# Chunked scan, rotation and output projection of a hybrid attention/HGRN2 layer: where the states, the rotation pieces and the last stage's instructions stand in order

## The chip, the cores and the metric

One core of one Trainium2 chip. The metric is device time in microseconds (us). The kernel before takes 2008.44 us, the median of 3 runs (2007.12 to 2008.82).

## The reference

One layer on 2048 latent tokens and 256 context tokens, model width 1024, float32. One input projection feeds two head groups, differential attention and a bidirectional HGRN2; both are gated, concatenated, projected, and added to the input under a LayerNorm:

```python
h_lat = x * (1.0 + scale) + shift
aq, ak, av, ag, hq, hi, hff, hfb, hg = _project(h_lat, w_in)     # 9 groups of 512 columns
q, k = _apply_rope(aq, cos, sin), _apply_rope(ak, cos, sin)      # rotation, latent tokens
p = softmax(q k^T / 8);  w = p[:, :, 0] - lam * p[:, :, 1];  attn = _rms_norm(w v) * 0.8
# HGRN2, forward and backward over the tokens, sum of both
S_t = diag(f_t) S_{t-1} + k_t v_t^T;  o_t = S_t^T q_t
y = concat([attn * silu(ag), _rms_norm(o_f + o_b) * silu(hg)]) @ w_out
x = _layer_norm(2 ** 0.25 * x + gate * y)
```

## The kernel before

Every float32 product is made of three products of halves (`hh`/`hl`, `wh`/`wl`: a rounded copy and the remainder), so one 128x512 result of depth 1024 takes 8 x 3 = 24 matmuls of 512 columns. The program has four stages in the profiled execution: input projections from 0 to about 920 us, into which the forward scan is merged from about 250 us; the last `aq`/`ak`/`hg` projections merged with the backward scan, 920 to 1092 us; attention, 1092 to 1803 us; the output projection of the last 14 of 16 tiles of 128 tokens, 1803 us to the end (2006.6 us).

**Projection and rotation.** `project_cols` (L469) issues 24 matmuls (L478) per bank of four called `pd`, and yields after every three. `evac_cols` empties the bank on ScalarE (L521, or L565 for `aq`/`ak`) into tiles called `e`. For `aq`/`ak` the rotation follows: `evac_scores` (L541) does a product at once or puts it into `self.deferred`. Its closure `rest` (L579) holds seven VectorE operations (L580, L581, L583, and twice L550 and L551) with four stores. `flush` (L465) runs everything deferred at one point, halfway through the next bank's matmuls (L480).

**Scan.** `merge` runs three steps of the projection, 9 matmuls, and then one step of the scan. The latent tokens form 8 groups (`NGRP`) of 256 tokens for each of two pairs of heads. The forward part of a group (`hgrn_group`, L640) goes through seven levels, in each of which four matmuls (L694) read what VectorE left (L695, L702). For the backward direction it stores three tiles of 256 KB: the decayed queries `QB` (L712), the state increments `UB` (L739) and the forward outputs `OP` (L754). `hgrn_backward` (L756) loads the three again for each group, in falling order of the groups. A step makes two products (L769) with the state `Sb`, then the next state by `state` (L632, L636), and a second step does the same for the other chunk; in a third step VectorE adds the bank to the forward outputs (L774) and the sum is stored to `Od`. State tiles have two buffers for each name, the banks `pm` too.

**Output projection.** For tile t, `front` (L217) loads gates `G` and mixed heads `Od`, squares on ScalarE (L1231), reduces on VectorE (L1234), scales by `rs` on POOL (L1240), transposes on TensorE (L1248), gates, rounds and takes the remainder on VectorE, VectorE and POOL (L1249, L1250, L1251). `back` makes 48 matmuls (L1272) and the residual and LayerNorm (L1275 to L1301, the last on POOL). `run` calls them tile after tile; a scheduler sets each engine's order. All DMAs are issued from one queue (SP), stores and loads alike.

Of the kernel before, what the change touches and what calls it, by code (L numbers as in the profile page):

```python
# [29 lines left out]
P = 128  # L30
D = 1024
# [87 lines left out]
class Build:  # L119
# [217 lines left out]
    def project_rest(self, att):  # L337
# [13 lines left out]
        yield from self.project(LAST_UNITS[:4], [0, 1])  # L351
        self.scores_projected = True
# [112 lines left out]
    def flush(self):  # L465
        while self.deferred:
            self.deferred.pop(0)()

    def project_cols(self, u, w, b, hb):  # L469
# [3 lines left out]
        for ct in range(2):  # L473
            ps = self.acc()
            cs = slice(ct * P, ct * P + P)
            for k in range(KT):
# [3 lines left out]
                if k == KT // 2:  # L480
                    self.flush()
# [59 lines left out]
    def evac_scores(self, kind, i, b, ps, n):  # L541
# [7 lines left out]
        def split(x, spare, half):  # L549
            nc.vector.tensor_copy(out=spare, in_=x)  # L550
            nc.vector.tensor_tensor(out=x.bitcast(F32R), in0=x, in1=spare.bitcast(F32), op=ALU.subtract)  # L551
            for d, src in zip(dst, (spare, x)):
                self.store(d[u].rearrange("(g t j) n -> t g j n", t=2, j=32)[half][:, :, ts], src.bitcast(F32))

        if b == NBLK:
            x, spare = tile("e1").bitcast(F32), tile("e2")
            nc.scalar.copy(out=x, in_=ps)
            self.deferred.append(lambda: split(x, spare, half))
            return
# [19 lines left out]
        def rest():  # L579
            nc.vector.tensor_tensor(out=xf, in0=xf, in1=cos, op=ALU.mult)  # L580
            nc.vector.tensor_tensor(out=p1f, in0=p1f, in1=pf, op=ALU.subtract)  # L581
            split(p1f, p, 0)
            nc.vector.tensor_tensor(out=x1f, in0=x1f, in1=xf, op=ALU.add)  # L583
            split(x1f, x, 1)

        self.deferred.append(rest)


    def hgrn(self):
# [4 lines left out]
        self.tot_b = {}  # L594
# [7 lines left out]
        loaded, active, finished = [], [], set()  # L602
# [29 lines left out]
    def state(self, S, d, u, tot, U):  # L632

        n = self.hg.tile([P, 2, P], F32, name=f"S{d}{u}", bufs=2)
# [5 lines left out]
    def hgrn_group(self, u, i, S):  # L640
# [67 lines left out]
        if latent:  # L708
# [3 lines left out]
            self.store(self.QBd[u][i], qq[:, 1, :, :])  # L712
# [9 lines left out]
        for d in range(2):  # L722
# [5 lines left out]
            t = hg.tile([P, 2, 2, P], F32, name="U%d" % d)  # L728
# [10 lines left out]
        self.store(self.UBd[u][i], U[1])  # L739
# [12 lines left out]
        op = hg.tile([P, 2, 2, P], F32, name="op", bufs=1)  # L752
        nc.scalar.copy(out=op, in_=po)
        self.store(self.OPd[u][i], op)  # L754

    def hgrn_backward(self, u, i, S, n):  # L756
        nc, hg, ph = self.nc, self.hg, self.ph
        tile = lambda nm, bufs: hg.tile([P, 2, 2, P], F32, name=nm, bufs=bufs)
        tags = ((("hq", 3), ("hv", 3), ("fb", 3)), (("km", 2), ("A", 2), ("kk", 3)))[n % 2]
        qb, ub, op = (tile(*x) for x in tags)  # L760
        qb = qb.rearrange("p a b t -> p a (b t)")
        self.load(qb, self.QBd[u][i])
        self.load(ub, self.UBd[u][i])
        self.load(op, self.OPd[u][i])
# [330 lines left out]
class Output:  # L1095
    def __init__(self, b):
        self.b, self.nc = b, b.nc
        self.gated = {}

# [90 lines left out]
    def run(self, out):  # L1190
# [9 lines left out]
        for t in range(2):  # L1200
            for _ in self.backs[t]:
                pass
        for t in range(2, NT):
            for _ in range(5 if t + 2 < NT else 0):
                self.advance(t + 2)
            for n in self.back(t):
                if n == 1 and t + 1 < NT:
                    while self.advance(t + 1):
                        pass
# [109 lines left out]
```

## Time and profile before

| | |
|---|---|
| median of 3 runs | 2008.44 us |
| time of the profiled execution | 2008.39 us |
| span of the profiled execution | 2006.6 us |
| TensorE (PE) busy | 1901.3 us, 95% |
| VectorE (DVE) busy | 1426.1 us, 71% |
| ScalarE (ACT) busy | 903.4 us, 45% |
| POOL busy | 894.1 us, 45% |
| DMA | 286.95 MB, mean 143 GB/s |

A busy share is an average over the four stages. TensorE's idle time is what can be won, and it lies in a few places; so the place, the engine that released it, and the granted clock of that stretch are read together.

### The profile page before, as it was taken

How to read it: one execution, taken by the hardware profiler on the slowest of the kernel's cores; microseconds unless marked ns; L12 is line 12 of the kernel's file. 1: busy time of each engine (PE TensorE's matmuls, PEld its weight loads, DVE VectorE, ACT ScalarE, POOL GpSimd, SP SyncE). 2: the span in 40 equal slices, each digit the busy share in tenths (PEclk: the TensorE clock that was granted, in tenths of full speed). 3: DMA queues.
4: the chain of work that ended last, by engine and by line, in shares of the span. 5: the costliest groups of instructions: out<-in, count | busy, mean ns of one | idle time of the engine just before them, and what ended most of it. 6: DMA issues, size and time to landing. Idle time of an engine off the chain costs nothing.

```text
span 2006.6 us, 32053 instructions
## 1 busy us (share of the span) xinstructions
PE 1901.3 (95%) x11712; PEld 1686.6 (84%) x11712; DVE 1426.1 (71%) x3055; ACT 903.4 (45%) x1349; POOL 894.1 (45%) x663
## 2 busy tenths in 40 slices
PE   7999999999998999999879999999999999998897
PEld 5888988898787998877667999999999999887676
DVE  7763456546687465777544389999999999967778
ACT  5523222322222322322000079989988889842121
POOL 0000145335445343453100057778777776745543
PEclk9999999999999999999889999999999999999999
DMA  9895652442444633434557641242252121144442
GB/s 359 269 260 184 231 184 90 165 156 75 147 134 145 198 121 127 161 106 145 189 181 232 195 130 51 76 139 74 70 144 64 44 82 43 46 152 161 148 146 95
DMA packets 180205, 286.95 MB, mean 143 GB/s; under 512 B 16848, under 2 KB 109264, under 8 KB 178000
## 3 DMA queue, kind: packets, MB, share of 16 engines
q1 hardware_dynamic: 180048, 284.91, 44.5%
q8 instruction: 93, 1.52, 0.3%
q14 instruction: 64, 0.52, 0.1%
HBM read 187.85 MB, written 97.00 MB: 142 GB/s over the span
## 4 chain that ended last, share of the span: by engine, by line
PE 63%; DVE 14%; DMA 12%; issue 4%; ACT 3%; POOL 3%; SPq 1%; DVEq 0%; POOLq 0%; ACTq 0%
PE pd L478 16%; PE po L1060 9%; PE pd L497 8%; PE s L973 6%; PE s L974 6%; PE pt L1040 6%; PE pl L694 4%; DMA QLd<-e 2%; PE py L1272 2%; DVE wl L428 2%; DMA KLd<-e 1%; DVE wsh L368 1%; PE pm L726 1%; DMA wraw<-win 1%; DMA kh<-Od 1%
## 5 line engine op out<-in xcount | busy, mean ns | idle before, releaser
L988 DVE TENSOR_SCALAR_CACHE_REDUCE e<-s 128x512 f32<-128x512 f32 (+1 forms) x512 | 372.8, 751 | 31.7 <-PE s L974 31.2
L478 PE MATMUL pd<-hh,wl 128*128 128x512 f32 (+1 forms) x928 | 372.3, 401 | 3.2 <-ACT e L534 3.2
L478 PE MATMUL pd<-hh,wh 128*128 128x512 f32 (+1 forms) x928 | 355.6, 383 | 0.0
L478 PE MATMUL pd<-hl,wh 128*128 128x512 f32 (+1 forms) x928 | 355.5, 383 | 0.0
L1023 POOL TENSOR_TENSOR e<-e,e 128x768 f32<-128x768 f32 (+1 forms) x192 | 351.1, 1857 | 2.6 <-ACT e L1016 0.2
L997 ACT ACTIVATE e<-e,nm 128x2304 f32<-128x2304 f32 x128 | 286.5, 2238 | 2.4 <-DVE nm L992 2.1
L973 PE MATMUL s<-kh,q 128*128 128x512 f32 (+1 forms) x640 | 244.4, 388 | 1.2 <-DMA q<-QHd 0.9
L974 PE MATMUL s<-kl,q 128*128 128x512 f32 (+1 forms) x640 | 231.4, 371 | 0.0
L699 POOL TENSOR_TENSOR kk<-kk,fb 128x512 f32<-128x512 f32 x126 | 170.5, 1355 | 134.4 <-DMA kk<-KD 101.3
L478 PEld LDWEIGHTS pd<-hh,wh 128*128 128x128 f32 x928 | 176.7, 190 | 34.3
L478 PEld LDWEIGHTS pd<-hh,wl 128*128 128x128 f32 x928 | 177.6, 191 | 31.0 <-ACT e L534 3.6
L478 PEld LDWEIGHTS pd<-hl,wh 128*128 128x128 f32 x928 | 177.6, 191 | 27.3
L689 ACT COPY km<-kk 128x512 f32<-128x512 f32 x112 | 70.9, 634 | 262.7 <-POOL kk L699 173.9
L1040 PE MATMUL pt<-eye,e 128*128 128x128 f32 x1152 | 162.8, 272 | 4.0 <-DVE w3l L1047 1.9
L1018 POOL TENSOR_SCALAR e<-e,cf 128x1280 f32<-128x1280 f32 x64 | 86.3, 1348 | 177.3 <-ACT e L997 73.5
L705 POOL TENSOR_TENSOR fb<-fb 128x512 f32<-128x512 f32 (+4 forms) x126 | 83.2, 661 | 162.5 <-DVE qq L702 148.0
L1040 PEld LDWEIGHTS pt<-eye,e 128*128 128x128 f32 x1152 | 135.7, 140 | 22.9 <-POOL e L1023 3.1
L694 PE MATMUL pl<-qq,km 128*128 128x128 f32 x896 | 131.1, 291 | 25.2 <-DVE qq L702 22.9
L694 PEld LDWEIGHTS pl<-qq,km 128*128 128x128 f32 x896 | 122.4, 196 | 38.2 <-issue 26.4
L497 PE MATMUL pd<-wh,hl 128*128 128x256 f32 x512 | 149.2, 291 | 1.1 <-ACT wh L427 1.1
L497 PE MATMUL pd<-wl,hh 128*128 128x256 f32 x512 | 145.4, 284 | 0.3 <-DVE wl L428 0.3
L497 PE MATMUL pd<-wh,hh 128*128 128x256 f32 x512 | 145.2, 284 | 0.0
(276 smaller groups left out, 4354.6 us busy)
## 6 DMA issues: line engine op xcount, KB each, us to landing
wraw<-win SPq DMA_DIRECT2D x68, 512.0 KB
xst<-xT SPq DMA_DIRECT2D x24, 512.0 KB
fb<-FD SPq DMA_DIRECT2D x18, 512.0 KB
kk<-KD SPq DMA_DIRECT2D x18, 512.0 KB
kh<-KHd SPq DMA_DIRECT2D x16, 576.0 KB
wsh<-wshift SPq DMA_DIRECT2D x16, 512.0 KB
wsh<-wscale SPq DMA_DIRECT2D x16, 512.0 KB
FD<-e SPq DMA_DIRECT2D x32, 256.0 KB
```

What stands on the lines that cost most here:

```text
L478: nc.tensor.matmul(ps[:, 0:n], a[:, k, cs], r[:, k, :], start=(k == 0 and j == 0), stop=(k == KT - 1 and j == 2))
L497: nc.tensor.matmul(ps[:, t, :], a[:, k, ts], r[:, k, :], start=(t == 0 and k == 0 and j == 0), stop=(t == 1 and k == KT - 1 and j == 2))
L694: nc.tensor.matmul(pl[:, e, ch, :], km[:, e, ch * P:ch * P + P], qm, start=True, stop=True)
L699: nc.gpsimd.tensor_tensor(out=o, in0=o, in1=total(fb, 1, 0, c), op=ALU.mult)
L973: nc.tensor.matmul(ps[:, c:c + w], q[:, m, :], kh[m][:, a + c:a + c + w], start=True, stop=False)
L974: nc.tensor.matmul(ps[:, c:c + w], q[:, 2 + m, :], kl[:, a + c:a + c + w], start=False, stop=True)
L988: self.nc.vector.tensor_scalar(out=d[e][:, a:b], in0=d.pop(("s", m, i)), scalar1=1.0, scalar2=None, op0=ALU.mult, op1=ALU.max, accum_out=s ...
L997: self.nc.scalar.activation(out=e, in_=e, func=AF.Exp, bias=self.tiles[t]["nm%d" % m], scale=1.0, accum_out=self.small(t, "z%d" % m))
L1018: self.nc.gpsimd.tensor_scalar(out=e, in0=e, scalar1=d["cf"], scalar2=1.0, op0=ALU.mult, op1=ALU.mult)
L1023: self.nc.gpsimd.tensor_tensor(out=d["e0"][:, a:b], in0=d["e0"][:, a:b], in1=d["e1"][:, a:b], op=ALU.add)
L1040: self.nc.tensor.transpose(out=ps[:, k - a, :], in_=d["e0"][:, k * P:k * P + P], identity=self.b.eye)
L1060: nc.tensor.matmul(out, a[:, k - _GROUPS[g][0], :], w[:, :, k - _GROUPS[g][0], :], start=(op == self.value_ends[0] and k == k0 and j == 0) ...
```

## The change

First, `flush` takes a number: from the second of a bank's eight steps on, one deferred piece is run per step and all that is left at the last; the closure `rest` is cut into seven pieces. Second, group 7 (`NGRP - 1`), the last of the forward scan and the first of the backward, keeps its three tiles on chip: six stores and six loads of 256 KB go. A backward group makes both its states in a step of their own, then its four products in the next; the state tiles take turns between the names `Sf` and `Sb`, which gives four buffers. Third, the output projection's instructions of TensorE, ScalarE, VectorE and the SP queue are written in order: `tile` places the next tile's transposes after 12 and 18 of the tile's 48 matmuls. From tile 4 on ScalarE squares with an accumulator (eight times 128 columns) and scales (eight more), and rounds; VectorE takes the remainder and does the LayerNorm in two products of 1024 columns; POOL does nothing. The front of tiles 2 and 3 stays as it was.

```diff
-    def flush(self):
-        while self.deferred:
+    def flush(self, n=None):
+        for _ in range(len(self.deferred) if n is None else min(n, len(self.deferred))):
             self.deferred.pop(0)()
...
-                if k == KT // 2:
-                    self.flush()
+                if k > 0:
+                    self.flush(1 if k < KT - 1 else None)
...
-        self.deferred.append(rest)
+        self.deferred += [times(xf, xf, cos), times(p1f, p1f, pf, ALU.subtract), *split(p1f, p, 0),
+                          times(x1f, x1f, xf, ALU.add), *split(x1f, x, 1)]
...
+        name = d
+        if d == "b" and ("f", u, NGRP - 1) in self.finished:
+            name = "fb"[self.turns[u] // 2 % 2]
+            self.turns[u] += 1
+        n = self.hg.tile([P, 2, P], F32, name=f"S{name}{u}", bufs=2)
...
-        self.store(self.OPd[u][i], op)
+        if i < NGRP - 1:
+            self.store(self.OPd[u][i], op)
+        else:
+            self.kept[u] = qq[:, 1, :, :], U[1], op
...
+        if i == NGRP - 1:
+            qb, ub, op = self.kept[u]
...
+        yield
+        tb, before = self.tot_b[u, i], {}
+        for c in (1, 0):
+            before[c] = S["b", u]
+            if i > 0 or c > 0:
+                self.state(S, "b", u, [tb[:, e, c:c + 1] for e in range(2)], ub[:, c, :, :])
         yield
         ps = ph.tile([P, 2, 2, P], F32, name="pm")
         for c in (1, 0):
             for e in range(2):
-                nc.tensor.matmul(ps[:, c, e, :], qb[:, e, c * P:c * P + P], S["b", u][:, e, :], start=True, stop=True)
-            if i > 0 or c > 0:
-                tb = self.tot_b[u, i]
-                self.state(S, "b", u, [tb[:, e, c:c + 1] for e in range(2)], ub[:, c, :, :])
-            yield
+                nc.tensor.matmul(ps[:, c, e, :], qb[:, e, c * P:c * P + P], before[c][:, e, :], start=True, stop=True)
+        yield
...
+        with self.b.tc.manual_schedule(engines={nc.tensor.engine, nc.scalar.engine, nc.vector.engine, nc.sync.engine}):
...
+    def tile(self, t):
...
+        products(half)
+        if before:
+            next(before)
+        if nxt:
+            self.gates(t + 1, 0)
+        products(2)
+        if nxt:
+            self.gates(t + 1, 1)
+        if before:
+            next(before, None)
+        if last:
+            return
+        products(2)
+        if nxt:
+            self.rest(t + 1)
+        next(back)
+        if t + 2 < NT:
+            self.norms(t + 2)
+        if t + 3 < NT:
+            self.fetch(t + 3)
+        products(KT)
...
+        for i in range(2 * H):
+            nc.scalar.activation(out=sq[:, i, :], in_=o[:, i, :], func=AF.Square, accum_out=ms[:, i:i + 1])
+        nc.scalar.activation(out=ms, in_=ms, func=AF.Sqrt, scale=1.0 / P, bias=self.b.eps)
+        nc.vector.reciprocal(out=rs, in_=ms)
+        for i in range(2 * H):
+            nc.scalar.activation(out=o[:, i, :], in_=o[:, i, :], func=AF.Copy, scale=rs[:, i:i + 1])
```

**VectorE in the backward scan, groups 7 to 5.** `Sf`/`Sb` on the left are new states (each row does both heads), `hv` and `A` the loaded increments; `fb`, `kk`, `op` are the sums of a bank `pm` with the forward outputs, and rows with `e` and `xst` (the rotation's sines and cosines) the rotation. Before:

```order
L636 SCALAR_TENSOR_TENSOR Sb_8296<-Sb_8250,tb_7_7947,hv 128x128 x2
L774 TENSOR_TENSOR fb<-pm,fb 128x512
L636 SCALAR_TENSOR_TENSOR Sb_8392<-Sb_8296,tb_6_7255,hv 128x128 x2
L580 TENSOR_TENSOR e_8302<-e_8302,xst 128x512
L581 TENSOR_TENSOR e_8227<-e_8227,e_8303 128x512
L583 TENSOR_TENSOR e_8226<-e_8226,e_8302 128x512
L550 CAST e_8303<-e_8227 128x512
L550 CAST e_8302<-e_8226 128x512
L551 TENSOR_TENSOR e_8227<-e_8227,e_8303 128x512
L551 TENSOR_TENSOR e_8226<-e_8226,e_8302 128x512
L636 SCALAR_TENSOR_TENSOR Sb_8362<-Sb_8339,tb_7_8127,A 128x128 x2
L774 TENSOR_TENSOR kk<-pm,kk 128x512
```
Now:

```order
L641 SCALAR_TENSOR_TENSOR Sb_8431<-Sf_8316,tb_6_7428,A 128x128 x2
L641 SCALAR_TENSOR_TENSOR Sb_8374<-Sb_8371,tb_6_7255,hv 128x128 x2
L794 TENSOR_TENSOR op<-pm,op 128x512
L641 SCALAR_TENSOR_TENSOR Sf_8491<-Sb_8374,tb_5_6645,hv 128x128 x2
L559 TENSOR_TENSOR e_8284<-e_8284,xst 128x512
L559 TENSOR_TENSOR e_8216<-e_8216,e_8285 128x512
L559 TENSOR_TENSOR e_8215<-e_8215,e_8284 128x512
L556 CAST e_8285<-e_8216 128x512
L556 CAST e_8284<-e_8215 128x512
L553 TENSOR_TENSOR e_8216<-e_8216,e_8285 128x512
L553 TENSOR_TENSOR e_8215<-e_8215,e_8284 128x512
L641 SCALAR_TENSOR_TENSOR Sb_8434<-Sb_8431,tb_6_7428,A 128x128
```
The first states of a group no longer stand between its own products: `Sf_8491` (group 5) is ahead of the seven rotation rows that follow, where `Sb_8362` (group 7) stood behind them. On TensorE a group is 4 products and then 27 matmuls of the projection, where it was 2, 9, 2 and 18.

**VectorE in the forward scan, the run of seven rotation operations that ends just ahead of TensorE's wait at 553.73 us.** `A` and `qq` are the scan's rows that TensorE waits for. Before:

```order
L580 TENSOR_TENSOR e_4852<-e_4852,xst 128x512
L581 TENSOR_TENSOR e_4783<-e_4783,e_4853 128x512
L583 TENSOR_TENSOR e_4782<-e_4782,e_4852 128x512
L550 CAST e_4853<-e_4783 128x512
L550 CAST e_4852<-e_4782 128x512
L551 TENSOR_TENSOR e_4783<-e_4783,e_4853 128x512
L551 TENSOR_TENSOR e_4782<-e_4782,e_4852 128x512
L695 COPY_PREDICATED A<-masks,pl 128x512
L702 TENSOR_TENSOR qq<-qq,fb 128x2x64x4
```
Now:

```order
L559 TENSOR_TENSOR e_4852<-e_4852,xst 128x512
L559 TENSOR_TENSOR e_4783<-e_4783,e_4853 128x512
L559 TENSOR_TENSOR e_4782<-e_4782,e_4852 128x512
L556 CAST e_4853<-e_4783 128x512
L700 COPY_PREDICATED A<-masks,pl 128x512
L553 TENSOR_TENSOR e_4783<-e_4783,e_4853 128x512
L707 TENSOR_TENSOR qq<-qq,fb 128x2x64x4
L556 CAST e_4852<-e_4782 128x512
L556 CAST e_4908<-e_4907 128x256
L553 TENSOR_TENSOR e_4782<-e_4782,e_4852 128x512
```
The scan's two rows have moved up by three and by two of the seven operations; at the next run of seven the rows stand as before.

**POOL at the start of the last stage.** `e<-e,rs` is the scaling of tile 3, `q<-q,lnb` the end of tile 0's LayerNorm, and `kl`, `e` of 512 columns the remainders. Before:

```order
L1240 TENSOR_TENSOR kh_18211<-kh_18211,rs 128x1024
L1251 TENSOR_TENSOR kl_18339<-kh_18211,kl_18339 128x512 x2
L1240 TENSOR_TENSOR e_18297<-e_18297,rs 128x1024
L1301 TENSOR_TENSOR q_18038<-q_18038,lnb 128x1024
L1301 TENSOR_TENSOR e_18260<-e_18260,lnb 128x1024
```
Now:

```order
L1397 TENSOR_TENSOR kh_18193<-kh_18193,rs 128x1024
L1408 TENSOR_TENSOR kl_18321<-kh_18193,kl_18321 128x512 x2
L1458 TENSOR_TENSOR q_18020<-q_18020,lnb 128x1024
L1397 TENSOR_TENSOR e_18279<-e_18279,rs 128x1024
L1458 TENSOR_TENSOR e_18242<-e_18242,lnb 128x1024
```
The scaling of tile 3, on which its transposes wait, has moved behind the end of tile 0's LayerNorm; on TensorE those transposes now stand after 12 of tile 2's matmuls, and what stands behind them there comes later.

## Rows read from the trace of the kernel before

**Rows 1.** Busy time by stretch: length, PE, PEld, DVE, ACT, POOL, clock, DMA share, GB/s.

```profile
920.00:1092.00 172.00, 146.28 (x697) 121.75 (x696) 89.53 (x186) 15.55 (x27) 18.18 (x18) 0.92 0.60 194
960.00:970.00 10.00, 4.76 (x13) 3.98 (x14) 5.17 (x13) 0.60 (x1) 0.00 (x0) 0.50 0.66 230
1803.00:1999.00 196.00, 174.21 (x828) 142.04 (x825) 155.78 (x225) 37.59 (x54) 96.44 (x54) 0.97 0.43 142
1820.00:1827.00 7.00, 6.26 (x15) 4.95 (x16) 5.23 (x9) 2.74 (x4) 4.27 (x3) 0.52 0.52 158
```

**Rows 2.** Waits of PE: line waited for, us in total, times, longest us.

```profile
PE pl L694 <- DVE qq L702: 22.9, 14, 5.1
PE pm L769 <- DVE Sb L636: 15.1, 3, 9.3
PE py L1272 <- POOL e L1251: 14.3, 6, 5.4
...
PE pm L769 <- DVE fb L774: 7.2, 2, 6.0
```

**Rows 3.** PE's timeline, backward scan: start us, us, operation, idle before and releaser.

```profile
965.24 1.23 PE L769 MATMUL pm<-Sb,km 128*128 128x128 f32 x4 [9.31 <-DVE Sb L636]
...
1008.23 0.80 PE L769 MATMUL pm<-Sb,hq 128*128 128x128 f32 x2 [5.29 <-DVE Sb L636]
...
1029.39 1.22 PE L769 MATMUL pm<-Sb,hq 128*128 128x128 f32 x4 [6.03 <-DVE fb L774]
```

**Rows 4.** The chain that ended last, 925 to 1095 us: start us, us, what.

```profile
954.53 10.28 DMA A<-UB
...
993.30 13.19 DMA QLd<-e
```

**Rows 5.** ACT's timeline, backward scan.

```profile
1006.59 1.09 ACT L565 ACTIVATE e<-pd 128x512 f32<-128x512 f32 x2 [18.11 <-DMA QLd<-e]
```

**Rows 6.** DVE's timeline in the forward scan.

```profile
549.80 2.58 DVE L551 TENSOR_TENSOR e<-e,e 128x512 fp32r<-128x512 f32 x2
552.30 0.71 DVE L695 COPY_PREDICATED A<-masks,pl 128x512 f32<-128x512 uint32 x1
```

**Rows 7.** PE's timeline, same place.

```profile
553.73 1.62 PE L694 MATMUL pl<-qq,km 128*128 128x128 f32 x6 [5.09 <-DVE qq L702]
```

**Rows 8.** PE's timeline, starts of tiles 3, 6, 7 and 15.

```profile
1820.74 0.79 PE L1272 MATMUL py<-woh,e 128*128 128x512 f32 x1 [5.35 <-POOL e L1251]
...
1861.86 0.50 PE L1272 MATMUL py<-woh,kl 128*128 128x512 f32 x1 [1.80 <-POOL kl L1251]
...
1876.05 0.50 PE L1272 MATMUL py<-woh,e 128*128 128x512 f32 x1 [1.99 <-POOL e L1251]
...
1987.10 0.28 PE L1272 MATMUL py<-woh,e 128*128 128x256 f32 x1
```

**Rows 9.** POOL's timeline, start of the last stage.

```profile
1805.66 1.90 POOL L1240 TENSOR_TENSOR e<-e,rs 128x1024 f32<-128x1024 f32 x1 [3.49 <-DVE rs L1239]
1808.86 2.38 POOL L1301 TENSOR_TENSOR q<-q,lnb 128x1024 f32<-128x1024 f32 x1 [1.30 <-DMA Od<-oa]
```

**Rows 10.** DVE's timeline, same stretch.

```profile
1807.40 1.24 DVE L1300 TENSOR_TENSOR q<-q,lng 128x1024 f32<-128x1024 f32 x1 [1.88 <-DMA lng<-lng]
```

**Rows 11.** ACT's groups, attention: shapes, count, then busy us, mean ns, idle before.

```profile
L997 ACT ACTIVATION_READ_ACCUMULATOR e<-e,nm 128x1 f32 x128 | 25.9, 203 | 0.0
...
L1081 ACT ACTIVATE oa<-pt,rz 128x128 f32<-128x128 f32 x62 | 19.3, 369 | 1.7 <-PE pt L1077 1.7
...
L1121 ACT CAST woh<-G 128x512 fp32r<-128x512 f32 x8 | 4.9, 607 | 0.0
```

**Rows 12.** All engines' groups, 1840 to 1990 us, same columns.

```profile
L1276 DVE SCALAR_TENSOR_TENSOR y<-x,y 128x512 f32<-128x512 f32 x22 | 29.1, 1324 | 0.4
...
L1300 DVE TENSOR_TENSOR y<-y,lng 128x1024 f32<-128x1024 f32 x11 | 13.5, 1226 | 14.7 <-ACT y L1299 14.7
...
L1249 DVE TENSOR_TENSOR e<-pt,G 128x512 f32<-128x512 f32 x12 | 8.2, 679 | 0.0
```

More of the change, by code (lines that the diff above doesn't have):

```diff
@@ L549, in split, with lower, times @@
         def split(x, spare, half):
[L550 to L553, printed above, removed]
+            def lower():
+                nc.vector.tensor_tensor(out=x.bitcast(F32R), in0=x, in1=spare.bitcast(F32), op=ALU.subtract)
+                for d, src in zip(dst, (spare, x)):
+                    self.store(d[u].rearrange("(g t j) n -> t g j n", t=2, j=32)[half][:, :, ts], src.bitcast(F32))
+            return [lambda: nc.vector.tensor_copy(out=spare, in_=x), lower]
+        def times(out, a, b, op=ALU.mult):
+            return lambda: nc.vector.tensor_tensor(out=out, in0=a, in1=b, op=op)
         if b == NBLK:
@@ L1098, in __init__ @@
         self.gated = {}
+        self.late = {}
     def open(self, stack):
@@ L1199, in run @@
             self.broadcast(nm, b.I[nm].unsqueeze(0), out)
-        for t in range(2):
-            for _ in self.backs[t]:
-                pass
[L1203 to L1209, printed above, removed]
+        nc = self.nc
+        with self.b.tc.manual_schedule(engines={nc.tensor.engine, nc.scalar.engine, nc.vector.engine, nc.sync.engine}):
+            for t in range(2):
+                for _ in self.backs[t]:
+                    pass
+            self.backs = {2: self.steady(2)}
+            self.fetch(4)
+            for t in range(2, NT):
+                self.tile(t)
+            for _ in self.backs[NT - 1]:
+                pass
@@ new lines, in tile @@
+    def tile(self, t):
+        back, before = self.backs[t], self.backs.get(t - 1)
+        nxt = t + 1 < NT
+        if nxt:
+            self.backs[t + 1] = self.steady(t + 1)
+        last = t == NT - 1
+        products = lambda n: [next(back) for _ in range(n)]
+        half = KT // 2 if not last else KT
+        products(half)
[11 more added lines that the diff above has]
+        products(2)
+        if nxt:
+            self.rest(t + 1)
[5 more added lines that the diff above has]
+        products(KT)
@@ new lines, in gates @@
+    def gates(self, t, half):
+        nc = self.nc
+        if t not in self.late:
+            while self.advance(t):
+                pass
+            return
+        g, w = self.late[t]
+        o, sq = (w[:, i * 2 * H:(i + 1) * 2 * H, :] for i in range(2))
+        if half == 0:
+            pool, na, nb = self.slots[t % 2]
+            gg = pool.tile([P, NKT, P], F32R, name=nb)
+            self.gated[t] = gg[:, 0:KT, :], gg[:, KT:2 * KT, :]
+        i = 4 * half
+        ps, gt = self.bank(), sq[:, i:i + 4, :]
+        for j in range(4):
+            nc.tensor.transpose(out=ps[:, j, :], in_=o[:, i + j, :], identity=self.b.eye)
+        nc.vector.tensor_tensor(out=gt, in0=ps, in1=g[:, i:i + 4, :], op=ALU.mult)
+        nc.scalar.copy(out=self.gated[t][0][:, i:i + 4, :], in_=gt)
```

111 lines of the change are left out of this document (90 added, 21 removed).

## Prediction

> **What bounds the kernel now.** I read the busy time by stretch first, then TensorE's waits, then its timeline at those waits, and last what its releasers waited for themselves. TensorE is busy 95% of the span, so only its gaps and its half-clock stretches can be won. The stretches show two places: in the backward scan TensorE works 146.28 of 172.00 us, at a mean granted clock of 0.92, and in the output stage 174.21 of 196.00 us [rows 1]. The list of waits names who ends them: VectorE's `qq` in the forward scan (22.9 us), VectorE's states and sums in the backward scan (15.1 and 7.2 us), POOL's remainder in the output stage (14.3 us for `e` alone) [rows 2]. Each is one part of the change.
>
> A gap costs twice. After the gap of 9.31 us that ends at 965.24 us [rows 3] the stretch 960 to 970 us has a granted clock of 0.50, the lower of the two levels, and after the 5.35 us at 1820.74 us [rows 8] the next 7 us have 0.52 [rows 1]. A matmul there takes about twice its time.
>
> **Backward scan.** All that can be won here is the idle time, 172.00 - 146.28 = 25.7 us, and the slow clock, (1 - 0.92) x 172.00 = 13.8 us [rows 1]. As some of the slow clock falls on idle time I take 37 us as the ceiling.
>
> What goes: six loads and six stores of 256 KB, 3 MB together. At the 194 GB/s of this stretch [rows 1] that is about 16 us of traffic; but the DMA engines are busy only 0.60 of the stretch, so it is worth nothing by itself, only where someone waits for it. Someone does: the chain has 10.28 us of a landing `A<-UB` [rows 4], after which VectorE makes the state that ends the gap of 9.31 us [rows 3]. With group 7 on chip the first states need no load, and the loads of group 6 are issued while group 7 is worked on. The second edit makes states a step ahead of the products; in VectorE's order group 5's state now precedes rotation work behind which group 7's stood. So of the 15.1 us on `Sb` [rows 2] I take 13 to go.
>
> What stays: the 6.03 us at 1029.39 us wait for the sum `fb` (L774) of another group, as there are two `pm` banks [rows 3]. The sum stands in VectorE's queue behind rotation rows, and these behind ScalarE, which waits 18.11 us at 1006.59 us for a store `QLd<-e` to land before it can empty a bank [rows 5]; the chain has such a landing with 13.19 us [rows 4]. The change does not shorten these landings except by the 3 MB. Of the 7.2 us on `fb` I take 2 to go. The clock: with about 15 of 25.7 us of gaps gone, half of the 13.8 us comes back, 7 us. Sum -22 us; bounds -37 (all of it goes) and -5 (only the first load wait, and another wait takes half of that).
>
> The added waits: a group's four products now come together, behind both states. They release in the order of the states, and a late state holds all four products and the 27 matmuls behind them, where before two products went ahead. That is in the lower bound. The extra buffers of the states cost nothing. Six fewer stores also leave SP, on which other issues queue; I count nothing for it beyond the landings.
>
> **Rotation in seven pieces.** In the forward scan L551's rows begin at 549.80 us, the scan's own row L695 follows at 552.30 us [rows 6], and TensorE idles 5.09 us until 553.73 us [rows 7]. At this place the order of the change moves the scan's two rows past three and two of the seven operations. Three operations are two of L551, 2.58/2 = 1.3 us each [rows 6], less for the one that stays ahead, and a cast: about 2 us sooner. But at the next run all seven still stand together. The scan's rows wait for TensorE's products in turn, so a shift in one place is only in part kept. Of the 22.9 us [rows 2] I take 3 us, and 1 us of clock: -4 us. Bounds: -9 (2 us at four of the 14 waits, and 1 us of clock) and +3 (the pieces now come between the scan's rows where these were in one run: one 1.3 us row at two or three places).
>
> **Output stage, steady part.** Tile 3 starts at 1820.74 us and tile 15 at 1987.10 us [rows 8]: 12 tiles in 166.4 us, 13.87 us each. Tile 6 starts at 1861.86 and tile 7 at 1876.05 us after an idle 1.99 us [rows 8], so a tile without a gap takes 14.19 - 1.99 = 12.2 us. The gaps wait for POOL, which does the remainder last. In the new order VectorE does it, and it has room: eight operations of 512 columns at 0.68 (row L1249), two more of the form L1276 at 1.32 and two of 1024 columns at 1.23 (row L1300) [rows 12], with half a us of small ones 11.0 us, and POOL no longer works beside it.
>
> ScalarE is the new partner. Per tile: eight squares of 128 columns, each at the price of L1081 and a read of the accumulator, 0.369 + 0.203 = 0.57, so 4.6 us; a root, taken like a scaling; eight scalings at 0.369, 3.0 us; two casts at 0.607, 1.2 us [rows 11]: 9.2 us. But it sits in a ring: transposes, gating, cast, second gating and cast, squares, root, reciprocal, scaling, and again transposes. With 0.5 us of transposes, 0.68 of gating, 1.9 until the second half, and the hops between engines, the ring is 11.7 to 12.5 us, as long as TensorE's own 12.2. I therefore take 12.6 us for a tile: 12 x (12.6 - 13.87) = -15 us. Bounds 12.2 (-20) and 13.2 (-8).
>
> The Trainium skill says in "ScalarE: Activation LUTs", section "Rules for kernel authors", that additions and multiplications belong on VectorE and not on ScalarE, which speaks against the scalings. By the same page, section "What ACT_TABLE_LOAD costs", I estimate a scaling of 128 columns at 186 + 93 + 0.833 x 128 = 386 ns, 93 less back to back; our row of 369 ns agrees with the single one, and with the overlap the ring would be 16 x 93 ns = 1.5 us shorter, a tile would go at TensorE's 12.2 us, and the sum would be 5 us lower, 1967 us.
>
> **Output stage, its start.** Here the change costs. TensorE's 13th matmul of tile 2 now comes behind transposes of tile 3, which wait for `e*rs` on POOL. This ran at 1805.66 us, 1.90 us long [rows 9]; in POOL's new order the end of tile 0's LayerNorm stands ahead of it, 2.38 us from 1808.86 us [rows 9], itself behind a product on VectorE which waits until 1807.40 us for the constants `lng` [rows 10]. So it ends at 1808.86 + 2.38 + 1.9 = 1813.1 us, and TensorE, with 12 matmuls done by about 1806, idles some 7 us, with slow clock behind. The other 36 matmuls and 8 transposes take 12.2 x 36/48 + 1 = 10, and 2 to 3 us for the clock: tile 3 starts at 1825 to 1826 us instead of 1820.74: +5 us (bounds +2 and +7). In the sum the old gap of 5.35 us is already left out, as it lay ahead of 1820.74. Tail after the last matmul: the same operations, 0.
>
> Stage: -15 + 5 = -10 us, bounds -18 and -1.
>
> **Sum.** -22 - 4 - 10 = -36 us on the execution's own 2008.39 us: 1972 us. The median of the runs, 2008.44 us, is the same within 0.1 us.
>
> **Rivals.**
>
> (A) The forecast, 1972 us, chance 0.5.
>
> (B) The backward scan clears entirely: -37 in place of -22, and the output ring keeps under 12.2 us (-15 in place of -10): 1952 us. For it: both state waits trace back to loads that go or come sooner. Against: the landings of 13.19 us [rows 4] stay. Chance 0.2.
>
> (C) The wait moves: the states are in time, but then TensorE stands for a free bank or for the sums, because ScalarE empties two banks after waits such as the 18.11 us of [rows 5], and then two in 1.09 us, while TensorE fills a pair in 48 matmuls, some 12 us. The backward scan gives 8 us or less: 2008.4 - 8 - 4 - 10 = 1986 us. For it: the landings. Against: not every bank waits so long. Chance 0.23.
>
> (D) Slower: ScalarE's ring becomes the bound of the output stage. The other parts give 26 us and the start takes 5, so the stage must lose 21 us in 12 tiles, 1.75 us each: from 13.87 + 1.75 = 15.6 us for a tile it decides. This needs 1.5 us per half more than the durations of [rows 11, 12], for instance each square and scaling at 0.57 + 0.2 and 0.37 + 0.2 (16 x 0.2 = 3.2 us). At 16 us the time is 2008.4 - 26 + 5 + 12 x 2.13 = 2013 us. Against: no row shows these prices. Chance 0.04. By the rule of the Trainium skill's "ScalarE: Activation LUTs" named above, the scalings in this ring are the mistake to look for.
>
> (E) The seven pieces change nothing (0 for -4): within (A), 1976 us. Chance 0.03 for all else, among it no net change.
>
> **How the numbers follow.** Likeliest is 1972. Leaving out (D), (E) and the far halves of (B) and (C), 8 in 10 lie from 1948 to 1993 us. A measurement of this kernel can tell 0.2%, 4 us, from no change. Faster by more: A, B, C = 0.93; within 4 us 0.03; slower 0.04.
>
> **What would show it.** Right: in the profile after, the waits of the four products on a state fall from 15 us to about 2; the mean clock of the backward stretch rises from 0.92 to 0.96 or more; tiles of the output stage 12.6 us apart; POOL idle there; a gap of about 7 us near 1806 to 1813 us of the old time line. The step on the backward scan is wrong if `pd` or `pm` waits for ScalarE or L774's sum take the place of the states (then C), that on the output stage if TensorE's transposes wait for the scalings (towards D), that on the rotation if waits on `qq` stay at 23 us.

## The result and the profile after

The changed kernel takes 1955.55 us, the median of 4 runs (1953.46 to 1957.15), against 2007.78 us for the kernel before (4 runs): a ratio of 0.9739, 95% interval 0.9723 to 0.9756. That is 52 us faster, inside the range given (1948 to 1993), 16 us below the forecast of 1972 and near rival B (1952). The profiled execution has a span of 1954.7 us, TensorE is busy 97%.

Where the time went is read from landmarks: the first start of an instruction that both kernels have. The first two come from a view by line (the last two numbers are the first and the last start), the others from TensorE's timeline (before, tiles 3 and 15 stand in [rows 8]). Before, then after:

```profile
L694 PE MATMUL pl<-qq,km x896: 270/275/553, 296.2 to 927.1; 128*128 128x128 f32 x180
L973 PE MATMUL s<-kh,q x640: 277/396/497, 1148.6 to 1760.5; 128*128 128x512 f32 x128, 128*128 128x256 f32 x32
...
1803.22 0.48 PE L1272 MATMUL py<-woh,kl 128*128 128x512 f32 x1
```

```profile
L699 PE MATMUL pl<-qq,km x896: 270/275/551, 297.0 to 925.3; 128*128 128x128 f32 x180
L993 PE MATMUL s<-kh,q x640: 277/396/628, 1117.5 to 1731.4; 128*128 128x512 f32 x128, 128*128 128x256 f32 x32
...
1774.42 0.48 PE L1338 MATMUL py<-woh,kl 128*128 128x512 f32 x1
...
1791.82 0.40 PE L1338 MATMUL py<-woh,e 128*128 128x512 f32 x1
...
1935.39 0.28 PE L1338 MATMUL py<-woh,e 128*128 128x256 f32 x1
```

| landmark | before | after | won up to here | won in this part | forecast |
|---|---|---|---|---|---|
| last product of the forward scan | 927.1 | 925.3 | 1.8 | 1.8 | 4 |
| first scores of the attention | 1148.6 | 1117.5 | 31.1 | 29.3 (backward scan) | 22 |
| tile 2 of the output | 1803.22 | 1774.42 | 28.8 | -2.3 (attention) | 0 |
| tile 3 | 1820.74 | 1791.82 | 28.9 | 0.1 (start of the last stage) | -5 |
| tile 15 | 1987.10 | 1935.39 | 51.7 | 22.8 (12 tiles) | 15 |
| end of the span | 2006.6 | 1954.7 | 51.9 | 0.2 (tail) | 0 |

TensorE's waits after, from the list of waits (line, releaser, us in total, times, longest), to be held against [rows 2]:

```profile
PE pl L699 <- DVE qq L707: 22.1, 14, 4.0
...
PE pm L792 <- DVE fb L794: 4.2, 2, 2.6
PE pt L1405 <- POOL e L1397: 3.6, 1, 3.6
...
PE pm L792 <- DVE kk L794: 2.7, 1, 2.7
```

The waits on `qq` have stayed (22.9, now 22.1 us). The wait of 15.1 us on the states `Sb` and the 14.3 us on POOL's remainder `e` are gone from the list; left in these two stages are sums of a bank (L794) and one wait on POOL at the start of the last stage. The busy time by stretch after, columns as in [rows 1]:

```profile
920.00:1080.00 160.00, 153.16 (x769) 129.26 (x768) 94.27 (x192) 17.57 (x30) 20.82 (x18) 1.00 0.65 206
1781.00:1791.00 10.00, 9.97 (x41) 8.42 (x42) 6.03 (x6) 0.00 (x0) 4.96 (x3) 0.83 0.60 199
1791.00:1947.00 156.00, 156.00 (x773) 129.70 (x771) 124.00 (x198) 80.07 (x337) 0.00 (x0) 1.00 0.47 164
```

In the backward scan the idle time fell from 25.7 to 160.00 - 153.16 = 6.8 us, and the mean granted clock rose from 0.92 to 1.00. So 18.9 us of the 29.3 us are idle time, and the rest, some 10 us, goes with the clock. From 1791 us to the end of the products TensorE does not pause at all; from tile 4 on the tiles are 11.91 us apart (tile 3 takes 12.52 us), where they were 13.87 us apart on average. The attention, which the change does not touch, took 2.3 us more; in eleven executions with the same code in that stage it took 654.3 to 658.2 us from its first scores to tile 2, so 2.3 us between two single executions don't show an effect of the change.

### The profile page after: what moved, and what is told of

Its sections match the earlier page's. It is cut to its first block, busy times and chain, and to the rows that moved or that the text cites. A ratio compares the mean times of both kernels' runs of the same rounds, so it can differ in the third digit from the quotient of the medians.

```text
span 1954.7 us, 32201 instructions
## 1 busy us (share of the span) xinstructions
PE 1888.6 (97%) x11712; PEld 1681.5 (86%) x11712; DVE 1404.4 (72%) x3043; ACT 948.0 (49%) x1636; POOL 812.2 (42%) x614
## 4 chain that ended last, share of the span: by engine, by line
PE 73%; DMA 9%; DVE 9%; issue 3%; POOL 3%; ACT 2%; SPq 1%; DVEq 0%; POOLq 0%; ACTq 0%
PE pd L479 17%; PE po L1080 10%; PE pd L498 9%; PE py L1338 8%; PE s L993 6%; PE s L994 6%; PE pt L1060 6%; PE pl L699 4%; DMA QLd<-e 2%; PE pm L732 1%; DVE wl L429 1%; DMA KLd<-e 1%; DVE wsh L369 1%; DVE qq L707 1%; DMA wraw<-win 1%
## 5 line engine op out<-in xcount | busy, mean ns | idle before, releaser
L699 PE MATMUL pl<-qq,km 128*128 128x128 f32 x896 | 130.2, 290 | 23.6 <-DVE qq L707 22.1
```

Of the source, the lines that this page charges most:

```text
L699: nc.tensor.matmul(pl[:, e, ch, :], km[:, e, ch * P:ch * P + P], qm, start=True, stop=True)
```

## The experiments

Twelve kernels ran, each the changed kernel with one edit (or two). Beside them stands the 1955.55 us of the changed kernel, and a ratio to the kernel before on the same chip (the changed kernel: 0.9739). Runs that leave a part of the program alone differ by some 2 us there, so differences under 3 us of the median are not read; landmarks of the profile are used for the smaller ones. The changed kernel didn't run again beside the twelve, and the fastest of them took 1957.6 us: a loss of 2 to 4 us in the median may be no loss at all.

**The output stage of the kernel before.**

```diff
-        with self.b.tc.manual_schedule(engines={nc.tensor.engine, nc.scalar.engine, nc.vector.engine, nc.sync.engine}):
-            ...
+        for t in range(2, NT):
+            for _ in range(5 if t + 2 < NT else 0):
+                self.advance(t + 2)
+            for n in self.back(t):
+            ...
```

> The change with the output stage of the kernel before, tiles 2 to 15; all else as changed. The profile after puts 22.8 us of the 51.9 us won between the starts of tiles 3 and 15 of that stage. If the three parts are separate in time, this run takes 1955.5 + 23 = 1978 us (1975 to 1982), and the backward scan and the attention end where they end in the changed kernel. If the output stage owes part of its gain to what comes ahead of it, less is lost, 1970 us or under.

1978.52 us, ratio 0.9845 (0.9827 to 0.9863): 23.0 us lost. From tile 3 on, tiles stand 12.07 to 14.52 us apart again. In the profiled execution, which is 5 us slower than the median, tiles 3 to 15 lose 21.4 us, and tile 2 starts 5.2 us later than in the changed kernel. So nearly all of the loss lies in the output stage, whose part is separate from the rest within these 5 us.

**Group 7 through memory again.**

```diff
...
-        if i == NGRP - 1:
-            qb, ub, op = self.kept[u]
-        else:
-            ...
+        self.load(qb, self.QBd[u][i])
+        self.load(ub, self.UBd[u][i])
+        self.load(op, self.OPd[u][i])
```

(and the three stores of group 7, in the lines left out)

> The change, but group 7 stores and loads its three tiles again, as all groups do. States stay a step ahead and keep four buffers. Theory 1, the forecast's: the first states waited for loads, so without group 7 on chip the backward scan loses 10 us or more of the 29.3 us that it gained: 1966 to 1972 us. Theory 2: states a step ahead of the products hide the loads as well; then it loses 4 us at most, 1959 us or under.

1977.78 us, ratio 0.9848 (0.9833 to 0.9863): 22 us lost, more than theory 1 asked for. The first scores come at 1136.5 us, 19 us later, though the forward scan ended at 923.9. VectorE's timeline in this run shows who is late:

```profile
937.44 0.61 DVE L641 SCALAR_TENSOR_TENSOR Sf<-Sb,tb,hv 128x128 f32<-128x128 f32 x2 [10.20 <-DMA hv<-UB]
960.36 0.62 DVE L641 SCALAR_TENSOR_TENSOR Sf<-Sb,tb,A 128x128 f32<-128x128 f32 x2 [12.57 <-DMA A<-UB]
```

and TensorE's what follows:

```profile
945.32 1.66 PE L752 MATMUL pm<-Sf,qq 128*128 128x128 f32 x4 [6.37 <-DVE Sf L641]
...
1023.42 1.22 PE L781 MATMUL pm<-Sb,hq 128*128 128x128 f32 x4 [9.36 <-DVE fb L783]
```

VectorE stands 10.20 and 12.57 us for the first two loads, with everything behind them in its queue: even a forward state, for which TensorE waits 6.37 us (`Sf`, first of TensorE's rows). States a step ahead do not hide this; they put VectorE in front of the load. The 9.36 us ahead of the later sum come from elsewhere. On VectorE that sum stands behind a row that waits for ScalarE, and ScalarE waits for a store to land (here, then in the changed kernel):

```profile
1021.39 0.60 ACT L522 ACTIVATE e<-pd 128x512 f32<-128x512 f32 x1 [21.36 <-DMA QLd<-e]
...
1022.02 0.75 DVE L528 SCALAR_TENSOR_TENSOR e<-pd,gains,e 128x512 f32<-128x512 f32 x1 [7.72 <-ACT e L522]
```

```profile
1001.69 0.60 ACT L522 ACTIVATE e<-pd 128x512 f32<-128x512 f32 x1 [17.43 <-DMA QLd<-e]
```

From the end of the forward scan to the first scores TensorE idles 12.5 us more than in the changed kernel, and the mean clock is 0.95 where it was 1.00. Whether the six extra loads are also what makes the landing late is not shown.

**The same, with the loads gone but the stores left in.**

```diff
-            if i < NGRP - 1:
-                self.store(self.QBd[u][i], qq[:, 1, :, :])
+            self.store(self.QBd[u][i], qq[:, 1, :, :])
...
-        if i < NGRP - 1:
-            self.store(self.UBd[u][i], U[1])
+        self.store(self.UBd[u][i], U[1])
```

> The change with the stores of group 7's queries and increments issued as before (four stores, 1 MB, which nobody reads); its loads stay away. The run with everything through memory lost 22 us. Theory: what it lost are the waits for the loads (VectorE's first states waited 10.20 and 12.57 us for them), so here little is lost: 1955.5 to 1958.5 us. Rival: the stores hold the queue and the DMA engines ahead of the first loads of group 6, then 5 us or more, 1961 us or over.

1959.34 us, ratio 0.9759 (0.9746 to 0.9773): 3.8 us, just above what was expected and far from 22. From the end of the forward scan (926.5) to the first scores (1121.1) it takes 194.6 us; in the changed kernel it is 192.2, in executions that differ from it only elsewhere 191.2 to 195.0, with group 7 through memory 212.6. So it is the loads that cost (with the stores of `OP`, which no run separates from them); what four stores of 256 KB cost does not stand out of this spread. The store of `OP` was left out here, as the sum is made in the same tile.

**States between the products.**

```diff
-        for c in (1, 0):
-            before[c] = S["b", u]
-            if i > 0 or c > 0:
-                self.state(...)
-        yield
...
+        for c in (1, 0):
+            for e in range(2):
+                nc.tensor.matmul(ps[:, c, e, :], qb[:, e, c * P:c * P + P], S["b", u][:, e, :], start=True, stop=True)
+            if i > 0 or c > 0:
+                self.state(...)
+            yield
```

> The change, but each backward group makes two products, a state, two products, a state, as before; group 7 stays on chip, the states keep their four buffers. Theory 1 (loads): little is lost, 5 us or less, 1960 us or under. Theory 2 (states ahead): 12 us or more are lost, 1967 us or over, and TensorE waits for states again (15.1 us in the kernel before, none now).

1960.81 us, ratio 0.9763 (0.9748 to 0.9777): 5.3 us lost. The first scores come at 1121.1 us, the forward scan ended at 924.0: 197.1 us between them, 4.9 more than 192.2 and 2.1 more than the longest execution with the states ahead and group 7 on chip. No wait on a state is in the list; the longest wait is for a sum:

```profile
PE pm L786 <- DVE fb L791: 8.5, 2, 7.1
```

A wait of the same length stands in the run with the stores left in, whose states are ahead:

```profile
1009.44 1.22 PE L790 MATMUL pm<-Sb,hq 128*128 128x128 f32 x4 [7.14 <-DVE fb L792]
```

In both, ScalarE's wait for the landing of `QLd<-e` ahead of it is longer than the 17.43 us of the changed kernel (19.87 us here, 21.93 us there). So this wait need not come from the order of the states. The median lies 0.3 us outside theory 1's 5 us and far from theory 2's 12, and the wait on states that theory 2 asked for is not there: theory 2 falls. Undone alone, the loads cost 20 us of the 29 and the order of the states 5 at most; the two undone together were not run, so how far the rest belongs to both, or to the four state buffers, stays open.

**Rotation at once.**

```diff
-                if k > 0:
-                    self.flush(1 if k < KT - 1 else None)
+                if k == KT // 2:
+                    self.flush()
```

> The change, but everything deferred of the rotation is issued at one point, halfway through the next bank, as before. The forward scan ends 1.8 us sooner in the changed kernel, so by the forecast (pieces matter only where they shift the scan's rows) this run takes 1957 to 1959 us. Rival: the pieces also keep the backward scan's states from standing behind seven rows in a row, then 1961 us or more, with new waits of the products there. Second rival: nothing at all, 1955.5 us within 1 us.

1959.22 us, ratio 0.9758 (0.9743 to 0.9772), 3.7 us in the median, just above the 1957 to 1959 us expected. The landmarks put little of it on the rotation: from the first to the last product of the forward scan (296.3 to 926.7) it takes 630.4 us, before 630.9, and in one execution each of the twelve kernels with the pieces 628.3 to 630.4, on average 629.2. The pieces seem worth 1 to 2 us, but there are only two executions without them, and the slowest with them is as slow. From there to the first scores it takes 192.1 us, as in the changed kernel (192.2), so the rival on the backward scan falls.

**The old fronts in the written order.**

```diff
-            self.norms(t + 2)
+            for _ in range(4 if t + 2 > 3 else 0):
+                self.advance(t + 2)
```

(and `advance` for `fetch` and `gates`)

> The change with its written order, but tiles 4 to 15 are prepared by the operations of the kernel before: squares of 1024 columns on ScalarE, the reduction on VectorE, scaling and remainder on POOL, rounding on VectorE. Transposes stay after 12 and 18 of the tile's matmuls. If the order makes the gain, a tile still takes 11.9 us and the run 1956 us (within 3 us). If the move of work off POOL makes it, VectorE and POOL slow each other and a tile takes 13 us or more: 12 x 1.1 = 13 us, 1969 us or over.

1978.22 us, ratio 0.9857 (0.9831 to 0.9882): 22.7 us lost, a tile takes 13.4 to 13.5 us. The order, with the LayerNorm on VectorE, makes 0.4 of the 1.96 us for a tile. The new preparation of a tile, off POOL and in pieces, makes the other 1.5 us; no run separates the two. The reason given was wrong: POOL's scaling takes 1.90 us as in the kernel before [rows 9], so this is no mutual slowing but a chain that is too long. TensorE's waits in this run, then one tile's links on VectorE, ScalarE and POOL:

```profile
PE pt L1410 <- POOL e L1402: 11.7, 7, 3.6
PE pt L1410 <- POOL kh L1402: 8.6, 6, 2.3
```

```profile
1861.73 1.20 DVE L1396 TENSOR_REDUCE ms<-e 128x8 f32<-128x1024 f32 x1
1862.96 0.30 ACT L1398 ACTIVATE ms<-ms,eps 128x8 f32<-128x8 f32 x1 [8.19 <-DVE ms L1396]
1863.30 0.20 DVE L1401 RECIPROCAL rs<-ms 128x8 f32<-128x8 f32 x1 [0.37 <-ACT ms L1398]
1863.58 1.90 POOL L1402 TENSOR_TENSOR e<-e,rs 128x1024 f32<-128x1024 f32 x1 [4.91 <-DVE rs L1401]
```

The tile starts at 1861.20 us and its 12 matmuls end at 1863.9; the scaled heads are there at 1865.5. The wait moved from the remainder to the scaling.

**Squares twice.**

```diff
+        for i in range(2 * H):
+            nc.scalar.activation(out=sq[:, i, :], in_=o[:, i, :], func=AF.Square, accum_out=mj[:, i:i + 1])
```

> The change with ScalarE's eight squares and accumulations of each of tiles 4 to 15 done twice, the first into a spare tile. In the profile after, one square comes every 0.295 us, 2.36 us for eight; the root ends at 1861.30 us and the scalings start at 1863.93 us, after 2.63 us in which ScalarE waits for VectorE's reciprocal. Theory: that reciprocal, which stands behind the first half's epilogue on VectorE, sets the ring, and the extra squares lie in that wait: 1956 us (within 2 us), the wait before the scalings falls to about 0.3 us. Rival, the forecast's: ScalarE's work sets the ring, then 12 x 2.1 = 25 us more, 1980 us.

1959.28 us, ratio 0.9758 (0.9736 to 0.9781), 1.3 us above what was expected. The tiles stay 11.91 us apart, and the wait ahead of the scalings falls from 2.63 to 0.29 us, as the theory said. So doubled squares don't lengthen a tile: in the changed kernel the wait for VectorE's reciprocal, and not ScalarE's squares, decides when the scalings start. After, and in this run:

```profile
1861.00 0.30 ACT L1281 ACTIVATE ms<-ms,eps 128x8 f32<-128x8 f32 x1
1863.93 2.46 ACT L1284 ACTIVATE kh<-kh,rs 128x128 f32<-128x128 f32 x8 [2.63 <-DVE rs L1282]
```

```profile
1866.12 0.30 ACT L1284 ACTIVATE ms<-ms,eps 128x8 f32<-128x8 f32 x1
1866.71 2.46 ACT L1287 ACTIVATE kh<-kh,rs 128x128 f32<-128x128 f32 x8 [0.29 <-DVE rs L1285]
```

What it lost lies at one place: tile 3 takes 16.71 us instead of 12.52, since tile 4 is the first to be prepared in the new way and its scalings come late by the doubled squares: TensorE idles 2.42 us ahead of its transposes, and part of the tile runs at a lower clock.

**Scalings twice.**

```diff
+        for i in range(2 * H):
+            nc.scalar.activation(out=o[:, i, :], in_=o[:, i, :], func=AF.Copy, scale=self.one)
```

> The change with eight more scalings (by 1.0) of 128 columns behind the eight of each of tiles 4 to 15, ahead of the transposes; eight take 2.46 us in the profile after. There the scalings end at 1866.39 us and the transposes start at 1866.71 us, so the slack is 0.3 us. Theory: 2.46 - 0.3 = 2.1 us more for each of 12 tiles, 25 us, 1980 us (1975 to 1985), with TensorE's transposes waiting for ScalarE. Rival: the loop is looser than this, then under 1965 us.

1964.0 us, ratio 0.9785 (0.9761 to 0.9808): a miss. A tile takes 12.16 us, 0.25 more and not 2.1. The eight took 1.69 us, but that explains little; the slack of 0.3 us had been read between the last scaling and the first transposes, which need only the first four. Each of these needs only its own scaling: the four transposes now take 0.87 us instead of 0.60 us, which is the 0.25 us of the tile (this run, then the changed kernel):

```profile
1862.91 0.87 PE L1305 MATMUL pt<-eye,e 128*128 128x128 f32 x4
```

```profile
1866.71 0.60 PE L1302 MATMUL pt<-eye,kh 128*128 128x128 f32 x4
```

More of the 8.5 us lies in tile 3, which takes 17.00 us instead of 12.52.

**Scalings three times.**

```diff
+        for i in [*range(2 * H), *range(2 * H)]:
+            nc.scalar.activation(out=o[:, i, :], in_=o[:, i, :], func=AF.Copy, scale=self.one)
```

> The change with 16 more scalings by 1.0 of each of tiles 4 to 15, where the run with 8 more lost only 0.25 us for a tile. Theory, formed on that run: a transpose waits for its own 128 columns alone, so the first four wait for the fourth scaling of the last round; in the run with 8 more this came 1.69 + 0.85 - 1.23 + 0.77 = 2.1 us later for 0.25 us lost, so the slack is 1.8 us. Another 8 are 1.69 us more, all of it on TensorE's way: 11.91 + 0.25 + 1.7 = 13.9 us for a tile, 12 x 1.7 = 20 us over that run's 1964.0, 1984 us (1979 to 1989). Rival: the loop shifts with the load and gives way again, then 12.5 us or less for a tile, under 1970 us.

1981.95 us, ratio 0.9873 (0.9859 to 0.9886). A tile takes 13.77 us (13.9 expected), and the list of waits has the scalings in it:

```profile
PE pt L1305 <- ACT kh L1287: 11.9, 6, 5.2
PE pt L1305 <- ACT e L1287: 8.1, 6, 1.4
```

In the tile that starts at 1864.58 us TensorE's transposes begin at 1868.89 us, while ScalarE's 16 more scalings run until 1870.24 us: they don't wait for the whole row. So ScalarE's ring is a real bound. With the scalings twice the fourth scaling of the last round came 2.1 us later, for 0.25 us lost: in the changed kernel the bound is some 1.8 us off.

**Scalings twice, norms ahead of the epilogue.**

```diff
-        next(back)
         if t + 2 < NT:
             self.norms(t + 2)
+        next(back)
```

(and the eight more scalings of the run with the scalings twice)

> The scalings twice as in the run with eight more scalings, and the norms of the tile after next (squares, root, reciprocal, scalings) are written ahead of the first half's epilogue. The root ends at 1861.30 us and VectorE's remainder at 1861.74 us, where the epilogue now ends at 1863.71 us: the reciprocal comes 2.0 us sooner. Theory: that takes back nearly all, 2.46 - 0.3 - 2.0 = 0.2 us for each of 12 tiles, 1956 to 1960 us. Rival: ScalarE's work as such is the bound, then the time stays near that of the run with eight more scalings.

1959.74 us, ratio 0.9766 (0.9742 to 0.9791). A tile takes 11.91 us again: the 0.25 us is taken back, so the reciprocal's place in VectorE's order is a part of the ring. In the changed kernel TensorE has no gap that this could fill. Tile 3 takes 16.33 us, as in the other runs with more work ahead of tile 4.

**Tile 3's scaling on VectorE, and its transposes later.**

```diff
-        (nc.vector if t == 1 else nc.gpsimd).tensor_tensor(out=o, in0=o, in1=rs.unsqueeze(2).broadcast_to([P, NH, P]), op=ALU.mult)
+        (nc.vector if t in (1, 3) else nc.gpsimd).tensor_tensor(out=o, in0=o, in1=rs.unsqueeze(2).broadcast_to([P, NH, P]), op=ALU.mult)
```

> The change with tile 3's scaling by rs on VectorE instead of POOL, where it stood behind the end of tile 0's LayerNorm. In the profile after the scaling runs from 1779.08 to 1780.98 us and TensorE idles 3.59 us until 1781.03 us, with a clock of 0.83 in the 10 us behind. On VectorE it can run at 1777.8 for 1.23 us: TensorE goes on at about 1779.1, 1.9 us sooner, and less slow clock: 1952 to 1954 us against 1955.5. Rival: tile 2 is held by something else (its own residual waits for x until 1792.44 us), then no difference, 1955.5 us within 1 us.

The second run has this edit and one more:

```diff
-        products(half)
+        late = t == 2
+        products(half + 2 * late)
...
-        products(2)
+        products(2 - late)
```

> As the run with tile 3's scaling on VectorE, and in tile 2 the transposes of tile 3 come after 18 and 21 of the matmuls instead of 12 and 18. The scaling ends at about 1779.1 us, 18 matmuls at 1774.4 + 18 x 0.2285 = 1778.5 us: the gap falls to 0.6 us and the clock stays up: 1955.5 - 3.0 - 1.7 = 1951 us (1949.5 to 1953). Rival: the later transposes make tile 3 wait for its gating and remainders on VectorE and POOL at its start, which take back what the gap gave: 1954 us or more.

1957.6 us, ratio 0.9750 (0.9737 to 0.9763), and 1958.36 us, ratio 0.9755 (0.9741 to 0.9768): nothing won, both expectations missed. TensorE's gaps in the first run, then in the second:

```profile
1780.55 1.09 PE L1405 MATMUL pt<-eye,e 128*128 128x128 f32 x8 [2.82 <-DVE e L1397]
1796.00 1.21 PE L1302 MATMUL pt<-eye,kh 128*128 128x128 f32 x4 [1.77 <-ACT kh L1284]
```

```profile
1779.98 1.09 PE L1406 MATMUL pt<-eye,e 128*128 128x128 f32 x8 [1.45 <-DVE e L1398]
...
1795.50 1.35 PE L1303 MATMUL pt<-eye,kh 128*128 128x128 f32 x4 [4.75 <-ACT kh L1285]
```

The gap ahead of tile 3's transposes shrinks from 3.59 to 2.82 and 1.45 us, and a new one opens ahead of tile 4's. Tiles 2 and 3 together take 31.0 and 33.2 us against 29.9. Two loads show why, that of tile 4's mixed heads (`kh<-Od`) and that of tile 2's residual (`x<-xn`). Here is the changed kernel, ScalarE and VectorE, then the SP queue:

```profile
1791.10 0.31 ACT L1280 ACTIVATE kh<-kh 128x128 f32<-128x128 f32 x1 [10.69 <-DMA kh<-Od]
...
1792.44 0.69 DVE L1327 SCALAR_TENSOR_TENSOR y<-x,y 128x512 f32<-128x512 f32 x1 [5.18 <-DMA x<-xn]
```

```profile
1784.54 0.34 SPq L128 DMA_DIRECT2D out<-e  x1
...
1785.54 0.88 SPq L125 DMA_DIRECT2D kh<-Od  x1
...
1786.47 0.48 SPq L125 DMA_DIRECT2D x<-xn  x1
```

ScalarE's squares for tile 4 wait until 1791.1 us for the one load, VectorE stands until 1792.4 us for the other, and tile 4's reciprocal comes behind both, at 1793.92 us. Both loads are issued behind the store of tile 1's result, which waits for POOL's end of that LayerNorm. In the changed kernel the gap ahead of tile 3's transposes had covered these waits. In the first run they also came later: on VectorE tile 3's scaling took 2.38 us ahead of tile 1's LayerNorm, so that store left at 1785.85 us, 1.3 us later, and ScalarE's squares began at 1792.49 us. Issuing both loads ahead of that store is the edit that follows; it was not tried.

## Why the prediction was right, and where it was off

The direction and the range were right, each part gave a gain, and the places of the waits were read rightly. The likeliest case was 16 us too cautious, and the size is that of rival B (1952 us), with the backward scan not quite cleared and the output stage better than there. By its steps:

- **Backward scan, -22, measured -29.3.** Of the 15.1 us on states 13 were to go; all went. Of the waits on sums about 2 were to go, as happened: 7.2 us on `fb` [rows 2] and 2.1 on `kk` became 4.2 and 2.7. With a wait of 1.4 us on a forward state, which the prediction left out, the idle time fell by 18.9 us where about 15 were forecast. The other mis-sized term is the clock: half of 13.8 us, 7 us, was to come back; the clock is 1.00, and some 10 us came with it. What remained are gaps of at most 2.7 us, and after those the clock did not fall. The first-load mechanism was right: undone alone, it costs 20 of the 29.3 us. But in that run only 6.4 us of TensorE's waits are on a state behind the loads; the rest is the longer wait on a sum and the clock.
- **The wait moves to banks and sums (rival C).** It was there in small: 6.9 us on sums, and 8.5 us where the states stood between the products. Its releaser is the one that C names, ScalarE's wait for a landing (17.43 us and more). It never took the 14 us that C needed.
- **Rotation, -4, measured about -1.4.** Right that the place at 553 us shifts: the wait there went from 5.09 [rows 7] to 3.34 us.

```profile
551.90 1.63 PE L699 MATMUL pl<-qq,km 128*128 128x128 f32 x8 [3.34 <-DVE qq L707]
```

  The waits on `qq` as a whole stayed, at 22.1 us; the prediction named a stay at 23 us as the sign that this step is wrong. The term that failed is the 3 us taken from them.
- **Steady tiles, -15, measured -22.8.** The step that failed is the ring of 11.7 to 12.5 us. It added durations of single instructions: a square 0.369 and a read of the accumulator 0.203, and 0.369 for a scaling [rows 11]. In the profile after, squares with their reads come every 0.295 us, and eight scalings take 2.46 us, 0.307 each:

```profile
1858.51 0.31 ACT L1280 ACTIVATE kh<-kh 128x128 f32<-128x128 f32 x1
1858.72 0.19 ACT L1280 ACTIVATION_READ_ACCUMULATOR kh<-kh 128x1 f32 x1
1858.82 0.29 ACT L1280 ACTIVATE kh<-kh 128x128 f32<-128x128 f32 x1
1859.02 0.19 ACT L1280 ACTIVATION_READ_ACCUMULATOR kh<-kh 128x1 f32 x1
```

  Instructions of one kind in a row overlap, and the price to add is the distance of their starts. The ring is thus 8 x (0.57 - 0.295) + 8 x (0.369 - 0.307) = 2.7 us shorter than forecast. Nor is ScalarE's work the whole way round the ring: the scalings wait 2.63 us for the reciprocal, and the first transposes need four scalings, not eight. TensorE's own time for a tile had also been put too high, at 12.2 us; it is 11.91. By the Trainium skill, "ScalarE: Activation LUTs", section "What ACT_TABLE_LOAD costs", a scaling back to back is 386 - 93 = 293 ns as an estimate, and 0.307 us agrees; the sentence beside the forecast (5 us less) was nearer than the sum. The rule of the same page of the Trainium skill that multiplications go to VectorE did not decide here: the ring had 1.8 us to spare. The scalings were not tried on VectorE.
- **Start of the last stage, +5, measured -0.1.** The order on POOL was read rightly, and the gap is there (3.59 us, forecast 7). The failing step is the constant `lng`: VectorE's product waited for it until 4.2 us after tile 2's start before [rows 10], and the forecast kept that. In the changed kernel it ran 0.7 us after tile 2's start and waited for no load, so the scaling ended 6.6 us after that start, not 9.9. Its load left earlier (SP queue before, then after, and VectorE's product):

```profile
1800.99 0.61 SPq L125 DMA_DIRECT2D lng<-lng  x1
```

```profile
1757.86 0.42 SPq L125 DMA_DIRECT2D lng<-lng  x1
...
1775.09 1.22 DVE L1457 TENSOR_TENSOR q<-q,lng 128x1024 f32<-128x1024 f32 x1
```

  That is 2.2 us ahead of tile 2's start before and 16.6 us after. With the output stage of the kernel before put back it is 2.2 us again (1777.4 us, tile 2 at 1779.65 us). So the written order of that stage moved the load, an effect that the prediction put at nothing.
- **Slower by ScalarE's ring (rival D).** The mechanism exists, as the run with three times the scalings shows (13.77 us for a tile), but it has 1.8 us for each tile to spare.

## What to carry to other kernels

Add durations only for instructions that wait for each other; for a row of like instructions take the distance of their starts, and for an engine's loop ask which piece the next engine needs first. Where this scan turns round, the first loads after the turn had nothing to hide behind, and keeping the turn's data on chip was worth more than reordering the work around it. A gap at the start of a stage may cover another one: before removing it, look at what the other engines wait for behind it.

## What was not expected of the hardware

The gaps of up to 2.7 us left in the backward scan had no lower clock behind them (1.00 over 160 us), where those of 9.31 and 5.35 us of the kernel before had 0.50 and 0.52 [rows 1]. It is no sharp rule: one execution of the changed kernel has 0.93 in a stretch of the attention (1699.59 to 1722.91 us) with gaps of 0.56 and 1.91 us, and the kernel before has 1.00 in the same work with the same gaps:

```profile
1699.59:1722.91 23.32, 20.86 (x132) 18.08 (x132) 21.28 (x59) 17.02 (x24) 15.52 (x11) 0.93 0.24 74
```

```profile
1730.20:1751.97 21.77, 19.30 (x132) 16.92 (x132) 21.01 (x59) 16.94 (x24) 15.54 (x11) 1.00 0.26 80
```

That alone is 1.6 us between two executions, and a reason not to read differences of this size. In the run with the squares twice, the gap of 2.42 us ahead of tile 4's transposes, no longer than those of the backward scan, is followed by a clock of 0.61 from 1798 to 1802 us:

```profile
1795.78 1.20 PE L1305 MATMUL pt<-eye,kh 128*128 128x128 f32 x4 [2.42 <-ACT kh L1287]
...
1798.00:1802.00 4.00, 4.00 (x14) 3.23 (x14) 2.36 (x5) 2.15 (x9) 0.00 (x0) 0.61 0.00 0
```
